# Halved matmul operands stored by even and odd tokens and read in turn, in a macaron decoder trunk on one Trainium2 core

## The chip, the cores and the metric

The kernel runs on one core of one Trainium2 chip. The metric is the device time of the whole program in microseconds (us), the median of several executions. Where engines are named, PE is TensorE's matmul side and PEld its weight loading, DVE is VectorE, ACT is ScalarE, POOL is GpSimd, and SP is the engine that issues most of the transfers.

## What is computed

Two layers, each made of a half-step SwiGLU feed-forward block, a mixer with three head groups, and a second half-step feed-forward block. There are 512 tokens, the model is 1024 wide and the feed-forward blocks 2816. Of the reference, what matters here:

```python
def swiglu(h, w_in, w_out):
    gate, up = jnp.split(h @ w_in, 2, axis=-1)
    return (jax.nn.silu(gate) * up) @ w_out
...
for l in range(DEPTH):
    x = x + 0.5 * swiglu(rms_norm(x, ffn1_norm[l]), ffn1_w_in[l], ffn1_w_out[l])
    h = rms_norm(x, mix_norm[l]) @ w_mix_in[l]
    (c_x, c_b, c_c, h_q, h_f, h_i, h_g, f_q, f_k, f_v, f_f) = jnp.split(h, split_at, axis=-1)
    y = jnp.concatenate([short_conv_mixer(...), hgrn2_mixer(...), fox_mixer(...)], axis=-1)
    x = x + y @ w_mix_out[l]
    x = x + 0.5 * swiglu(rms_norm(x, ffn2_norm[l]), ffn2_w_in[l], ffn2_w_out[l])
```

Everything is float32.

## The kernel before

**Three matmuls for one product.** Each float32 operand is split into a rounded part `hi` (type fp32r) and the rest `lo`; a product is then hi·hi + hi·lo + lo·hi, three fp32r matmuls into one accumulator. `mm3` (lines 423 to 437) issues the three, so its lines 428, 434 and 435 are most of the matmuls of the program. A matmul has a *stationary* operand of 128 columns, put into the array by a weight load that the profile lists as LDWEIGHTS under PEld, and a *moving* operand whose columns stream past it; both are read from SBUF, the on-chip memory. Each of the three matmuls has a weight load of its own, which runs while the matmul before it streams.

**Reading in turn.** `woven` (line 184) rewrites the moving operand: a row of 512 columns is read as column 0, column 256, column 1, column 257 and so on, two halves 1024 bytes apart read in turn. The accumulator then holds the columns in this order, and whoever reads the accumulator uses `unwoven` (line 194), which takes every second column, beside `halves` (line 189) for the tensor in ordinary order. `woven` does so only where the operand has T = 512 columns; narrower operands are read straight through.

**Halved products.** In the feed-forward blocks, most of both projections is computed by a seven-product scheme on 2x2 blocks: the tokens are cut into two halves of H = 256, the contraction and the features into two each, and sums and differences of the quarters are multiplied. The method `halved` (lines 825 to 1019) runs them; `plan` (line 66) writes out the order of the products and, for each place in it, which transfers, sums and operands are made there. One call of `product` (lines 907 to 917) is 2 feature groups by 4 contraction blocks by 3 matmuls, that is 24 matmuls, each with 256 moving columns. The stationary operands are weights: `prepare` makes their `hi` on ACT (line 882) and their `lo` on DVE (line 884) three products ahead, into one of three buffers named `hl`. The moving operands are of two kinds, both made once by `two` (lines 810 to 820), `hi` on ACT and `lo` on DVE: `xc`, seven per feed-forward block, from the normalised input quarters `xn` (made by `operand`), and `m`, fourteen per block, from the hidden quarters `hq` (made by `moving`). Before, each is a tile of 4 contraction blocks by 256 tokens in ordinary token order. With `follow`, the order of instructions on PE, ACT, DVE and SP around these products is set by hand: an instruction on an engine waits for the one before it in this order.

**Skew.** The buffer `hl` starts its contents 16 elements late where it is the stationary operand of a halved product (`SKEW_HELD`) and 48 elements late where it is a moving operand narrower than 512 columns (`SKEW_MOVING`).

**Mixer.** The 264 columns are the 256 columns of `H_I` (the values of the linear-recurrence heads) and the 8 columns of `F_F` (the forget gates of the attention heads), computed together at line 1162 with the tokens as the stationary and the weights as the moving operand, in four steps of two contraction blocks per layer. The weights of a step come by two transfers on SP's queue into one of two buffers `st` (`load_rows`, line 352), are split by lines 413 and 416, and the results are taken from the accumulators at lines 1169 and 1172.

**Last output.** The last feed-forward block leaves its result with tokens on the partitions, weights moving; the last tile of 512 columns is cut into two halves of 256 so that its end comes sooner (lines 616 to 656).

Of the kernel before, what the change touches and what calls it, by code (L numbers as in the profile page):

```python
# [182 lines left out]

def woven(x):

    return x.rearrange("p (h t) -> p t h", h=2) if x.shape[-1] == T else x


def halves(x):
# [9 lines left out]
class Trunk:  # L199
# [223 lines left out]
    def mm3(self, acc, ah, al, bh, bl, first, last, parted=False, keep=False):  # L423

        nc = self.nc
        n = bh.shape[-1]
        for c in (slice(0, n // 2), slice(n // 2, n)) if parted else (slice(0, n),):
            i = nc.tensor.matmul(  # L428
                acc[:, c], ah, woven(bh[:, c]), start=first and c.start == 0, stop=False,
                skip_group_check=True,  # L430
            )
            if keep:
                self.follow("p", i)
        nc.tensor.matmul(acc, ah, woven(bl), start=False, stop=False, skip_group_check=True)  # L434
        i = nc.tensor.matmul(acc, al, woven(bh), start=False, stop=last, skip_group_check=True)  # L435
        if keep:
            self.follow("p", i)

# [159 lines left out]
    def ffn(self, w_in, w_out, next_gain, covered, mean=None, begin=None, out=None):  # L598

        nc = self.nc
        tc = self.tc
        with tc.tile_pool(name=self.n("ffn"), bufs=1) as fp:
            self.tt, self.tb = "g2", 2
            if begin is not None:
                x, gain = begin
            self.hq = {}
            self.cover(fp, w_in, w_out, covered, mean, begin)

            f0, nf = CHUNKS[-1]
            if next_gain is not None:
                self.begin_norm(next_gain)
            last = out is not None
            self.ntog += 1
            if last:
                xs = []
                turn = self.turn_x(xs, (("mm", "mm"), ("sc", "pt"))[self.ntog % 2])
            for dg in range(2):
                banks = self.next4()  # L620

                def parts(k, kk, dg=dg):
                    r = slice((f0 + k) * P, (f0 + k + kk) * P)
                    return [w_out[r, dg * 512 : (dg + 1) * 512]]

                spans = [slice(c, c + P) for c in (0, 128, 256, 384)]
                jobs = [
                    (bk, slice(0, T), c) if last else (bk, c, None) for bk, c in zip(banks, spans)
                ]
                pieces = [[(bk, slice(0, T))] for bk in banks]  # L630
                if last and dg:

                    pieces[3] = [
                        (bk[:, : T // 2], slice(c, c + T // 2))
                        for bk, c in ((banks[3], 0), (self.next4()[0], T // 2))
                    ]
                    jobs[3:] = [(bk, c, spans[3]) for bk, c in pieces[3]]
                for _ in self.stream_steps(
                    jobs,
                    parts, lambda k: (self.hh[k // 2][:, k % 2, :], self.hl[k // 2][:, k % 2, :]), nf,  # L640
                ):
                    if last:
                        next(turn, None)
                if last:
                    for i in range(4):
                        o = self.xo[dg * 4 + i]
                        for bk, c in pieces[i]:
                            whole = c.stop - c.start == T
                            nc.vector.scalar_tensor_tensor(
                                out=halves(o[:, c]), in0=unwoven(bk) if whole else halves(bk),  # L650
                                scalar=0.5, in1=halves(xs[dg * 4 + i][:, c]),
                                op0=ALU.mult, op1=ALU.add,
                            )
                            nc.sync.dma_start(
                                out[0, spans[i], dg * T + c.start : dg * T + c.stop], o[:, c]
                            )
                    continue
                for i in range(4):
                    j = dg * 4 + i
                    xj = self.xT[:, j, :]  # L660
                    nc.vector.scalar_tensor_tensor(
                        out=halves(xj), in0=unwoven(banks[i]), scalar=0.5, in1=halves(xj),
                        op0=ALU.mult, op1=ALU.add,
                    )
                    if next_gain is not None:
                        self.norm_part(j, fp)
# [133 lines left out]
    def operand(self, fp, name):  # L800

        c = ORDER_IN.index(name)
        hi, lo = (
            fp.tile([P, 4, T // 2], F32R, tag=f"x{w}{c}", name=self.n("xc")) for w in "hl"
        )
        a, v = self.two(hi, lo, self.xn[SUM[name]], name in NEGATIVE)
        self.follow("a", a), self.follow("v", v)
        self.xc[name] = hi, lo

    def two(self, hi, lo, src, other):  # L810

        nc = self.nc
        if other:
            return (
                nc.scalar.activation(hi, src, AF.Copy, scale=-1.0),
                nc.vector.scalar_tensor_tensor(
                    out=lo, in0=src, scalar=-1.0, in1=hi, op0=ALU.mult, op1=ALU.subtract
                ),
            )
        return nc.scalar.copy(hi, src), nc.vector.tensor_sub(lo, src, hi)  # L820

    def halved(self, fp, w_in, w_out, covered, deal):
# [63 lines left out]
        def moving(c, p):  # L886

            hi, lo = (
                fp.tile([P, 4, H], F32R, tag=f"m{w}", name=self.n("m"), bufs=2) for w in "hl"
            )  # L890
            a, v = self.two(hi, lo, self.quarter(fp, c, *SUM[p]), p in NEGATIVE)
            A(a), V(v)
# [13 lines left out]

        def product(u, p, bank, start, stop, parted):
            hi, lo = parts.pop((u, p))
            xh, xl = self.xc[p] if u[0] == "I" else mov[u[1][0], p]
            for i in range(2):  # L910
                acc, c = bank[:, i * H : (i + 1) * H], slice(i * P, (i + 1) * P)
                for k in range(4):
                    self.mm3(
                        acc, hi[:, k, c], lo[:, k, c], xh[:, k, :], xl[:, k, :],
                        start and i == 0 and k == 0, stop and i == 1 and k == 3,
                        parted and i == 0 and k == 0, True,
                    )
# [158 lines left out]
    def mix(self, l, w, w_out, conv_w, out_gain, q_gain, k_gain, f_bias, next_gain, logits):  # L1076
# [3 lines left out]
        with tc.tile_pool(name=self.n("mix"), bufs=1) as mp:  # L1080
# [48 lines left out]
            with tc.tile_pool(name=self.n("hg"), bufs=1) as hp:  # L1129
# [28 lines left out]
                for i in range(2):  # L1158
# [2 lines left out]
                bv = [self.bank(t) for t in ("mm", "sc", "sc", "mm")]  # L1161
                self.stream(
                    [(bv[i][:, :264], slice(0, 264), TOK[i]) for i in range(4)],
                    cols((H_I, 256), (F_F, 8)), self.xact, KD,
                )
                v = hp.tile([P, 4, 256], F32, tag="v", name=self.n("v"))
                zf = mp.tile([P, 4, NH], F32, tag="zf", name=self.n("zf"))
                for i in range(4):
                    nc.scalar.activation(
                        v[:, i, :], bv[i][:, :256], AF.Copy, scale=self.invc[:, i : i + 1]  # L1170
                    )
                    nc.vector.scalar_tensor_tensor(
                        out=zf[:, i, :], in0=bv[i][:, 256:264], scalar=self.invc[:, i : i + 1],
                        in1=fb, op0=ALU.mult, op1=ALU.add,
                    )
                run = [
                    self.hgrn(l, pr, hp, z[pr], q[pr], v, sg[pr], og, S[pr], kb[pr], b[pr])
# [705 lines left out]
```

## Time and profile before

| | |
|---|---|
| median of 3 runs | 1788.92 us (1787.59 to 1790.13) |
| the profiled execution, its own time | 1787.5 us |
| its span in the profile | 1785.7 us |
| instructions in the profile | 33379 |
| bytes read from device memory over the span | 226.15 MB, 128 GB/s |

The page of the profile gives busy time by engine, then the span in 40 slices, the transfers, and the chain of work that ended last. Matmuls are pipelined: the time of one, as listed, runs from its start to the end of its last result, so it overlaps the next one, and the rate at which a stretch runs is read from the distance between the starts of successive matmuls. In the lists of groups a line reads: line of the kernel, engine, operation, what it writes and reads, partitions by elements, count, then the busy time of the group, the mean time of one in ns, and the engine's idle time before them with what ended it. In the view by windows each row has a stretch, its length, and for each engine the busy time with the number of instructions in brackets.

### The profile page before, as it was taken

How to read it: one execution, taken by the hardware profiler on the slowest of the kernel's cores; microseconds unless marked ns; L12 is line 12 of the kernel's file. 1: busy time of each engine (PE TensorE's matmuls, PEld its weight loads, DVE VectorE, ACT ScalarE, POOL GpSimd, SP SyncE). 2: the span in 40 equal slices, each digit the busy share in tenths (PEclk: the TensorE clock that was granted, in tenths of full speed). 3: DMA queues.
4: the chain of work that ended last, by engine and by line, in shares of the span. 5: the costliest groups of instructions: out<-in, count | busy, mean ns of one | idle time of the engine just before them, and what ended most of it. 6: DMA issues, size and time to landing. Idle time of an engine off the chain costs nothing.

```text
span 1785.7 us, 33379 instructions
## 1 busy us (share of the span) xinstructions
PE 1774.0 (99%) x13613; PEld 1659.7 (93%) x13613; DVE 1428.7 (80%) x1991; ACT 993.9 (56%) x1417; POOL 176.8 (10%) x174
## 2 busy tenths in 40 slices
PE   9999999999999999999999999999999999999999
PEld 7999999888888899999989999998878889999998
DVE  8889887678777888879678887876777779888883
ACT  5555555465666565555445555555656655555552
POOL 0011120100000101112001110201000000020210
PEclk9999999999999999999999999999999999999999
DMA  7668784243543857868276787823435438687762
GB/s 216 185 132 190 182 175 104 76 116 92 131 110 107 239 138 156 198 158 175 83 209 139 169 184 194 170 76 80 123 91 128 119 108 211 166 163 193 156 140 95
DMA packets 253114, 262.35 MB, mean 147 GB/s; under 512 B 23528, under 2 KB 232176, under 8 KB 252960
## 3 DMA queue, kind: packets, MB, share of 16 engines
q1 hardware_dynamic: 197104, 192.02, 35.7%
q0 software_dynamic: 55840, 68.19, 23.9%
q8 instruction: 107, 1.75, 0.4%
q14 instruction: 47, 0.39, 0.1%
q10 hardware_dynamic: 16, 0.00, 0.0%
HBM read 226.15 MB, written 2.17 MB: 128 GB/s over the span
## 4 chain that ended last, share of the span: by engine, by line
PE 87%; DVE 6%; ACT 4%; DMA 2%; issue 1%; SPq 0%; ACTq 0%; DVEq 0%
PE mm L428 13%; PE mm L435 12%; PE mm L434 12%; PE sc L428 6%; PE sc L435 6%; PE sc L434 6%; PE pt L428 6%; PE pt L434 6%; PE pt L435 6%; PE po L428 3%; PE po L434 3%; PE po L435 3%; DVE hl L416 2%; ACT hl L413 1%; DMA st<-in_ffn_w_in_dram 1%
## 5 line engine op out<-in xcount | busy, mean ns | idle before, releaser
L882 ACT CAST hl<-w 128x1024 fp32r<-128x1024 f32 x322 | 337.7, 1050 | 341.9 <-PE mm L435 83.1
L884 DVE TENSOR_TENSOR hl<-w,hl 128x1024 fp32r<-128x1024 f32 x322 | 392.6, 1220 | 83.1 <-ACT hl L882 82.9
L416 DVE TENSOR_TENSOR hl<-st,hl 128x1024 fp32r<-128x1024 f32 (+3 forms) x152 | 160.1, 1053 | 108.7 <-ACT hl L413 107.9
L413 ACT CAST hl<-st 128x1024 fp32r<-128x1024 f32 (+3 forms) x151 | 137.7, 912 | 166.3 <-PE po L435 78.4
L428 PE MATMUL mm<-xc,hl 128*128 128x256 f32 (+1 forms) x730 | 201.3, 276 | 0.3 <-ACT g L981 0.3
L435 PE MATMUL mm<-xc,hl 128*128 128x256 f32 x728 | 201.2, 276 | 0.0
L434 PE MATMUL mm<-xc,hl 128*128 128x256 f32 x728 | 201.1, 276 | 0.0
L428 PE MATMUL sc<-xc,hl 128*128 128x256 f32 (+1 forms) x530 | 146.4, 277 | 0.6 <-ACT g L981 0.6
L435 PE MATMUL sc<-xc,hl 128*128 128x256 f32 x528 | 146.1, 277 | 0.1
L434 PE MATMUL sc<-xc,hl 128*128 128x256 f32 x528 | 146.0, 277 | 0.0
L428 PEld LDWEIGHTS mm<-xc,hl 128*128 128x128 f32 x730 | 137.1, 188 | 0.8 <-ACT g L981 0.5
L435 PEld LDWEIGHTS mm<-xc,hl 128*128 128x128 f32 x728 | 136.7, 188 | 0.1
L434 PEld LDWEIGHTS mm<-xc,hl 128*128 128x128 f32 x728 | 136.7, 188 | 0.0
L434 PE MATMUL pt<-xc,hl 128*128 128x256 f32 x480 | 132.6, 276 | 0.0
L428 PE MATMUL pt<-xc,hl 128*128 128x256 f32 (+1 forms) x482 | 132.6, 276 | 0.0
L435 PE MATMUL pt<-xc,hl 128*128 128x256 f32 x480 | 132.5, 276 | 0.0
L428 PE MATMUL mm<-x,hl 128*128 128x512 f32 x272 | 105.9, 389 | 0.0
L435 PE MATMUL mm<-x,hl 128*128 128x512 f32 x272 | 103.1, 379 | 0.0
L434 PE MATMUL mm<-x,hl 128*128 128x512 f32 x272 | 103.1, 379 | 0.0
L428 PEld LDWEIGHTS sc<-xc,hl 128*128 128x128 f32 x530 | 99.5, 188 | 1.4 <-ACT g L981 1.0
L435 PEld LDWEIGHTS sc<-xc,hl 128*128 128x128 f32 x528 | 99.2, 188 | 0.3 <-DVE hl L884 0.3
L434 PEld LDWEIGHTS sc<-xc,hl 128*128 128x128 f32 x528 | 99.1, 188 | 0.0
(506 smaller groups left out, 5404.8 us busy)
## 6 DMA issues: line engine op xcount, KB each, us to landing
w<-in_ffn_w_in_dram SPq DMA_DIRECT2D x140, 512.0 KB, 5.4
w<-in_ffn_w_out_dram SPq DMA_DIRECT2D x64, 512.0 KB, 5.5
w<-in_ffn_w_out_dram POOLq DMA_DIRECT2D x56, 512.0 KB, 8.5
st<-in_w_mix_in_dram SPq DMA_DIRECT2D x80, 256.0 KB, 3.0
w<-in_ffn_w_in_dram POOLq DMA_DIRECT2D x39, 512.0 KB, 8.4
st<-in_ffn_w_in_dram SPq DMA_DIRECT2D x70, 256.0 KB, 3.6
w<-S POOLq DMA_DIRECT2D x35, 512.0 KB, 4.8
st<-in_ffn_w_out_dram SPq DMA_DIRECT2D x24, 512.0 KB, 3.6
```

The source lines that it names most:

```text
L413: a = nc.scalar.copy(hi, src[:, c : c + w])
L416: b = nc.vector.tensor_sub(lo, src[:, c : c + w], hi)
L428: i = nc.tensor.matmul(acc[:, c], ah, woven(bh[:, c]), start=first and c.start == 0, stop=False, skip_group_check=True,)
L434: nc.tensor.matmul(acc, ah, woven(bl), start=False, stop=False, skip_group_check=True)
L435: i = nc.tensor.matmul(acc, al, woven(bh), start=False, stop=last, skip_group_check=True)
L882: A(nc.scalar.copy(hi, src))
L884: return lambda: V(nc.vector.tensor_sub(lo, src, hi))
```

## The change

The moving operands `xc` and `m` are stored as two rows of 512: first all even tokens of all four contraction blocks, then all odd ones. `two` reads its source with a step of two elements for this and writes straight through. `product` views the operand as contraction block by token by half, and `mm3` reads it so that the two halves, 2048 bytes apart, come in turn; the columns then arrive in ordinary token order, and whoever reads these accumulators is unchanged. `woven` now applies to every moving operand that is a plain row of columns, whatever its width; so the 264 columns (halves 528 bytes apart) and the two last output halves (512 bytes apart) are read in turn as well, and their readers use `unwoven`. For the 264 columns the weights are brought in an order that puts half of `H_I` and half of `F_F` together, by four transfers a step.

```diff
 def woven(x):
 
-    return x.rearrange("p (h t) -> p t h", h=2) if x.shape[-1] == T else x
+    return x.rearrange("p (h t) -> p t h", h=2) if len(x.shape) == 2 else x
...
     def mm3(self, acc, ah, al, bh, bl, first, last, parted=False, keep=False):
 
         nc = self.nc
-        n = bh.shape[-1]
+        n = acc.shape[-1]
+        bh, bl = woven(bh), woven(bl)
         for c in (slice(0, n // 2), slice(n // 2, n)) if parted else (slice(0, n),):
             i = nc.tensor.matmul(
-                acc[:, c], ah, woven(bh[:, c]), start=first and c.start == 0, stop=False,
-                skip_group_check=True,
+                acc[:, c], ah, bh[:, c.start // 2 : c.stop // 2, :],
+                start=first and c.start == 0, stop=False, skip_group_check=True,
             )
             if keep:
                 self.follow("p", i)
-        nc.tensor.matmul(acc, ah, woven(bl), start=False, stop=False, skip_group_check=True)
-        i = nc.tensor.matmul(acc, al, woven(bh), start=False, stop=last, skip_group_check=True)
+        nc.tensor.matmul(acc, ah, bl, start=False, stop=False, skip_group_check=True)
+        i = nc.tensor.matmul(acc, al, bh, start=False, stop=last, skip_group_check=True)
...
                         for bk, c in pieces[i]:
-                            whole = c.stop - c.start == T
                             nc.vector.scalar_tensor_tensor(
-                                out=halves(o[:, c]), in0=unwoven(bk) if whole else halves(bk),
+                                out=halves(o[:, c]), in0=unwoven(bk),
...
         hi, lo = (
-            fp.tile([P, 4, T // 2], F32R, tag=f"x{w}{c}", name=self.n("xc")) for w in "hl"
+            fp.tile([P, 2, T], F32R, tag=f"x{w}{c}", name=self.n("xc")) for w in "hl"
         )
...
     def two(self, hi, lo, src, other):
 
         nc = self.nc
+        src = src.rearrange("p k t -> p (k t)").rearrange("p (n h) -> p h n", h=2)
         if other:
...
             hi, lo = (
-                fp.tile([P, 4, H], F32R, tag=f"m{w}", name=self.n("m"), bufs=2) for w in "hl"
+                fp.tile([P, 2, T], F32R, tag=f"m{w}", name=self.n("m"), bufs=2) for w in "hl"
             )
...
         def product(u, p, bank, start, stop, parted):
             hi, lo = parts.pop((u, p))
-            xh, xl = self.xc[p] if u[0] == "I" else mov[u[1][0], p]
+            xh, xl = (
+                x.rearrange("p h (k t) -> p k t h", k=4)
+                for x in (self.xc[p] if u[0] == "I" else mov[u[1][0], p])
+            )
...
-                        acc, hi[:, k, c], lo[:, k, c], xh[:, k, :], xl[:, k, :],
+                        acc, hi[:, k, c], lo[:, k, c], xh[:, k], xl[:, k],
...
                     [(bv[i][:, :264], slice(0, 264), TOK[i]) for i in range(4)],
-                    cols((H_I, 256), (F_F, 8)), self.xact, KD,
+                    cols((H_I, 128), (F_F, 4), (H_I + 128, 128), (F_F + 4, 4)), self.xact, KD,
                 )
...
                     nc.scalar.activation(
-                        v[:, i, :], bv[i][:, :256], AF.Copy, scale=self.invc[:, i : i + 1]
+                        halves(v[:, i, :]), unwoven(bv[i][:, :256]), AF.Copy,
+                        scale=self.invc[:, i : i + 1],
                     )
                     nc.vector.scalar_tensor_tensor(
-                        out=zf[:, i, :], in0=bv[i][:, 256:264], scalar=self.invc[:, i : i + 1],
-                        in1=fb, op0=ALU.mult, op1=ALU.add,
+                        out=halves(zf[:, i, :]), in0=unwoven(bv[i][:, 256:264]),
+                        scalar=self.invc[:, i : i + 1], in1=halves(fb), op0=ALU.mult, op1=ALU.add,
                     )
```

On every engine the same instructions stand in the same order as before; only SP's queue has more of them, eight transfers more in each layer.

## The prediction

> **What bounds the kernel now.** I read the busy shares first, then the chain that ended last.
>
> ```profile
> PE 1774.0 (99%) x13613; PEld 1659.7 (93%) x13613; DVE 1428.7 (80%) x1991; ACT 993.9 (56%) x1417; POOL 176.8 (10%) x174
> ...
> PEclk9999999999999999999999999999999999999999
> ...
> PE 87%; DVE 6%; ACT 4%; DMA 2%; issue 1%; SPq 0%; ACTq 0%; DVEq 0%
> ```
>
> PE is the bound, at the full granted clock throughout. Since busy matmuls overlap, 99% says only that PE rarely waits; what it could gain is in the spacing of starts. The halved products fill four stretches, one per feed-forward block:
>
> ```profile
> 76.50:305.20 228.70, 228.70 (x2018) 228.67 (x2017) 193.60 (x203) 128.33 (x145) 32.22 (x27) 1.00 0.71 158
> 616.80:865.70 248.90, 248.53 (x2185) 247.97 (x2184) 213.34 (x226) 140.04 (x160) 35.36 (x30) 1.00 0.71 158
> 939.40:1188.00 248.60, 248.29 (x2186) 247.84 (x2185) 212.39 (x225) 139.52 (x159) 34.43 (x29) 1.00 0.71 158
> 1498.40:1747.10 248.70, 248.39 (x2186) 248.00 (x2186) 213.44 (x225) 138.79 (x159) 35.32 (x30) 1.00 0.71 159
> sum 974.90, PE 973.92 PEld 972.48 DVE 832.76 ACT 546.69 POOL 137.33; mean PE 243.48 PEld 243.12 DVE 208.19 ACT 136.67 POOL 34.33
> ```
>
> The columns are PE, PEld, DVE, ACT, POOL. Together 2018 + 2185 + 2186 + 2186 = 8575 matmuls in 974.9 us, 113.7 ns each; PE idles 1 us in all, DVE is busy 85%, ACT 56%. Inside, the spacing is constant (timeline: start, length, both us):
>
> ```profile
> 119.95 0.28 PE L435 MATMUL po<-xc,hl 128*128 128x256 f32 x1
> ...
> 122.67 0.28 PE L435 MATMUL mm<-xc,hl 128*128 128x256 f32 x1
> ```
>
> That is 24 spacings in 2.72 us: 113.3 ns for 256 columns. The operands of 512 columns, already read in turn, do better per column:
>
> ```profile
> 354.69 0.38 PE L435 MATMUL mm<-x,hl 128*128 128x512 f32 x1
> ...
> 368.29 0.38 PE L435 MATMUL mm<-x,hl 128*128 128x512 f32 x1
> ```
>
> 63 spacings in 13.60 us: 215.9 ns for 512 columns, so 107.9 for 256. The question is whether those 113.3 ns belong to the order of reading.
>
> **Halved products: order of reading.** One place streams rows straight through with almost no weight load beside them (8 columns):
>
> ```profile
> 399.37 0.39 PE L1534 MATMUL pt<-utri,flh 128*8 128x512 f32 x1
> 399.60 0.40 PE L1534 MATMUL pt<-utri,fll 128*8 128x512 f32 x1
> ...
> 400.18 0.28 PE L1534 MATMUL pt<-utri,flh 128*8 128x256 f32 x1
> 400.29 0.28 PE L1534 MATMUL pt<-utri,fll 128*8 128x256 f32 x1
> 400.41 0.22 PE L1534 MATMUL pt<-utri,flh 128*8 128x128 f32 x1
> ```
>
> Straight through, 512 columns take 230 ns (399.37 to 399.60) against 215.9 in turn, and 256 take 115 (400.18 to 400.41, two). So straight reading costs 6 to 7% by itself, without a weight load to blame, and the 113.3 is of the same kind. I take it that reading in turn removes it.
>
> How far down? The stream itself allows half of 215.9, 107.9, if nothing in a matmul is fixed; what is fixed would add a little.
>
> The Trainium skill, "TensorE: Matmul & The Clock Gate", section "Wait — 56ns, not 53.3ns?", states columns over 2.4 GHz plus about 2.5 ns a matmul; the 215.9 agrees, and by it alone the halved products would run at 109.2 and gain 35 us.
>
> From the side of the weight load, which in the halved products never rests (two rows of the timeline, then two groups: count, busy us, mean ns):
>
> ```profile
> 519.15 0.23 PE L1714 MATMUL po<-PH,V 128*128 128x128 f32 x1
> 519.21 0.27 PE L1714 MATMUL po<-PL,V 128*128 128x128 f32 x1
> ...
> L1714 PE MATMUL po<-PL,V 128*128 128x128 f32 x32 | 8.8, 274 | 0.0
> L1714 PE MATMUL po<-PH,V 128*128 128x128 f32 x32 | 7.2, 224 | 0.0
> ```
>
> Here 128 columns stream for less time than a load takes: the second matmul starts 60 ns after the first and ends 60 + 274 - 224 = 110 ns after it, so back-to-back loads allow about 110 ns. Does reading in turn slow the load beside it?
>
> ```profile
> L428 PEld LDWEIGHTS mm<-xc,hl 128*128 128x128 f32 x730 | 137.1, 188 | 0.8 <-ACT g L981 0.5 <-issue 0.2
> L428 PEld LDWEIGHTS mm<-x,hl 128*128 128x128 f32 x272 | 51.5, 189 | 7.7 <-issue 1.0
> ```
>
> 188 ns beside straight reading, 189 beside reading in turn, and such a load lies within each of the 215.9 ns, beside the stream, as one would always do after the change. The trace has no pair 2048 bytes apart, only 1024. The slower of stream and load sets the pace, so I take the load's 110, less a little because its starts are given in steps of 10 ns: 109.6, and 8575 x (113.3 - 109.6) = 32 us. Bounds: 107.9 gives 46, 110 gives 28, and with the load at fault nothing.
>
> **What the writers pay.** `two` now reads every second element; ACT and DVE each do it for 32 + 24 + 16 + 12 = 84 operands:
>
> ```profile
> L820 ACT CAST m<-hq 128x1024 fp32r<-128x1024 f32 x32 | 33.4, 1044 | 2.8 <-DVE hq L897 2.8
> L815 ACT ACTIVATE m<-hq 128x1024 fp32r<-128x1024 f32 x24 | 25.2, 1051 | 0.0
> L820 ACT CAST xc<-xn 128x1024 fp32r<-128x1024 f32 x16 | 16.7, 1041 | 5.5 <-DVE xn L719 4.1 <-DVE xn L793 1.4
> L815 ACT ACTIVATE xc<-xn 128x1024 fp32r<-128x1024 f32 x12 | 12.7, 1059 | 8.5 <-DVE xn L719 5.5 <-DVE xn L793 3.0
> ...
> L324 ACT ACTIVATE lk<-lk 128x512 f32<-128x512 f32 x4 | 2.5, 635 | 6.0 <-DVE lk L1317 6.0
> L324 ACT ACTIVATE t<-lk 128x256 f32<-128x256 f32 x4 | 2.0, 588 | 0.0
> ```
>
> ```profile
> L1397 DVE TENSOR_TENSOR t<-t,q 128x256 f32<-128x256 f32 x4 | 1.5, 420 | 0.0
> L1404 DVE TENSOR_TENSOR t<-kb,b 128x256 f32<-128x256 f32 x20 | 8.3, 415 | 0.0
> ```
>
> On DVE the step of two costs nothing (L1397 reads and writes with that step, L1404 in runs). On ACT, `t<-lk` reads and writes with a step of two: 588 ns, where 256 straight elements would take some 430 (635 less 256 at the 0.80 ns between the 512 and the 1024 row). If all of that excess lies in the reading, an operand costs 4 x 158 = 0.63 us more. I take a quarter, 0.16, since half the stepping there is writing, and nothing shows a stepped read alone. In both cases ACT has room: at worst 84 x 0.63 = 53 us on 547. The wait falls on DVE, where `lo` stands right behind in the given order and everything after it waits too, the `lo` of the next weights first. DVE then has 833 + 53 = 886 us of 943, 94%; the three products that are prepared ahead cover that on the mean, and not everywhere. They already ran out once:
>
> ```profile
> 838.58 0.19 PEld L435 LDWEIGHTS sc<-xc,hl 128*128 128x128 f32 x1 [0.26 <-DVE hl L884]
> ```
>
> I set 3 us of PE waiting against the gain; bounds 0 and 15, the latter a quarter of the 53 plus 2.
>
> **The 264 columns.** 372.12 to 373.32 holds ten spacings:
>
> ```profile
> 372.12 0.28 PE L435 MATMUL sc<-hl,x 128*128 128x264 f32 x1
> ...
> 373.32 0.29 PE L428 MATMUL sc<-hl,x 128*128 128x264 f32 x1
> ```
>
> 120 ns each; at the 512 rate 111.3. With 96 a layer, 192 x 8.7 = 1.7 us gained, if PE is what waits last. Against it stands the queue of SP, with eight issues more a layer (a row of the timeline, then a group with ACT's idle time before it).
>
> ```profile
> 372.52 0.88 SPq L352 DMA_DIRECT2D st<-in_w_mix_in_dram  x2
> ...
> L413 ACT CAST hl<-st 128x528 fp32r<-128x528 f32 x8 | 4.9, 617 | 0.6 <-DMA st<-in_w_mix_in_dram 0.6
> ```
>
> An issue takes 0.44 us, so the last part of a step is issued 0.88 us later, and the loads of the next projection stand behind it. The cast already waited for such a transfer. Cost between 0 and 8 x 0.88 = 7 us; I take 2, most steps being loaded ahead. Net: nothing. The two last output halves are 36 matmuls:
>
> ```profile
> L428 PE MATMUL pt<-hl,hh 128*128 128x256 f32 x6 | 1.7, 284 | 0.0
> ```
>
> 36 x (284 - 271) = 0.5 us, 271 being 379 less 108. Their DVE readers take every second element of an accumulator, as those of the other banks do already.
>
> **Sum.** -32 + 3 + 0 - 0.5 = -29.5 us on the execution's own 1787.5, 1758. The shown median is 1.4 us higher than that execution: 1759.
>
> **Rivals.**
>
> *The load sets the 113.3 (no change).* PEld is 93% busy, and 113.3 is only 3 ns above what loads allow. Against it: the rows with 8-column loads show the cost of straight reading without a load. Time: 1789, to 1792 with the writers' waits. Chance 0.06; I count 113.3 to 112.9 here.
>
> *DVE takes over (half the gain).* Stepped reads cost ACT the full 0.63 us and DVE's order passes it on. For: DVE at 85%, above 90% where a block's operands are made. Against: lookahead of three products. Time: 1759 + 12 = 1771. Chance 0.13.
>
> *Reading in turn collides with the weight load (slower).* A load that never rests may meet both halves, which 512 columns with a load in only half of the time do not show. Price: straight rows of 256 against another placement of the weights run at 120 ns,
>
> ```profile
> 518.67 0.28 PE L1714 MATMUL po<-PH,V 128*128 128x256 f32 x1
> ...
> L1659 PE MATMUL sc<-S,S 128*128 128x256 f32 x8 | 2.7, 333 | 0.0
> ```
>
> four spacings in 0.48 us from there to the 519.15 above; so 8575 x 6.7 = 57 us more, 1846. The worst placement in the trace takes 333 ns a matmul, 57 over the 276 that the halved ones take; that would be 489 us. It decides as soon as the spacing ends above 113.3. Against it: 189 for the load, 215.9 for the stream, with both on. The Trainium skill, "SBUF — State Buffer", section "Specifications (TRN2)", speaks for this rival: lines have 16 bytes, and full bandwidth wants at least two hits per line, while reading in turn leaves the line at every element. By that rule 512 columns in turn should already be the slower ones; the trace has them at 215.9 against 230, so it does not hold for this stream. Chance 0.08.
>
> **Chances and range.** The forecast has 0.73: 1742 (spacing 107.9, no waits) to 1768 (spacing 110, waits at 8). With DVE taking over it reaches 1777. I leave out the slower rival and most of no change: 1746 to 1777. Faster by more than 0.2% (3.6 us, about what a measurement of this kernel can tell): 0.73 + 0.13 = 0.86, less 0.01 for waits that eat more than the gain; same 0.06; slower 0.08 + 0.01 = 0.09.
>
> **What would show it.** In the changed profile, 256-column matmuls of lines 428 to 436 at 271 or 272 ns instead of 276, their spacing 109 to 110, and stretches of about 241 us with the same counts; PEld still 188 to 190. For the writers, the `m` and `xc` casts on ACT between 1.04 and 1.68 us and DVE's wait for them (4.8 us for `m<-hq` in before); PE waiting for `hl` L884 in more than one place. For the mixer, 264-column spacing at 111 to 112 and the idle time of the 128x528 cast. I am wrong if the spacing stays above 112, or if it falls and PE waits for DVE take more than 10 us.

## The result, and the profile after

The changed kernel takes 1779.89 us (median of 6 runs, 1779.45 to 1781.39) against 1788.89 us for the kernel before in the same comparison: 9.0 us less, a ratio of 0.995 with a 95% interval of 0.9937 to 0.9963. That is faster by 0.5%, which a measurement of this kernel can tell from nothing, but less than a third of the 29.5 us that was forecast, and outside the range given. One execution in all that follows, the third of run 12, ran at a granted clock of 0.556 and took 3022.88 us; it is counted in that run's median of 1779.82 us, which is 1779.61 us without it, and not in its ratio.

The page of the changed kernel: busy shares, granted clock, chain that ended last.

```profile
PE 1761.0 (99%) x13613; PEld 1644.1 (92%) x13613; DVE 1439.3 (81%) x1991; ACT 1022.1 (57%) x1417; POOL 176.9 (10%) x174
...
PEclk9999999999999999999999999999999999999999
...
PE 81%; DVE 10%; ACT 5%; issue 2%; DMA 2%; SPq 0%; ACTq 0%; DVEq 0%
```

PE is still the bound at the full clock; ACT and DVE hold a little more of the chain. The four stretches of halved products, cut at the first and last start of a halved matmul in each kernel, by the view of busy time in windows (length, then PE, PEld, DVE, ACT, POOL). The changed kernel:

```profile
77.60:304.20 226.60, 226.26 (x2020) 225.67 (x2020) 195.80 (x203) 132.19 (x145) 32.23 (x27) 1.00 0.72 159
615.60:862.80 247.20, 245.48 (x2187) 244.54 (x2187) 215.70 (x227) 144.98 (x160) 36.45 (x31) 1.00 0.72 160
936.20:1183.10 246.90, 245.51 (x2188) 244.55 (x2187) 214.87 (x226) 144.49 (x160) 34.92 (x30) 1.00 0.71 160
1494.10:1741.40 247.30, 245.55 (x2188) 244.59 (x2187) 215.88 (x226) 143.81 (x159) 36.41 (x31) 1.00 0.71 160
sum 968.00, PE 962.79 PEld 959.35 DVE 842.25 ACT 565.48 POOL 140.01; mean PE 240.70 PEld 239.84 DVE 210.56 ACT 141.37 POOL 35.00
```

The kernel before, cut in the same way:

```profile
sum 976.10, PE 975.12 PEld 973.64 DVE 833.96 ACT 547.09 POOL 137.73; mean PE 243.78 PEld 243.41 DVE 208.49 ACT 136.77 POOL 34.43
```

The stretches are 8.1 us shorter, the three long ones some 247 us each in place of the 241 that were to show. PE now idles 5.2 us in them (968.00 less 962.79) where it idled 1.0. Two rows of the changed kernel's timeline give the spacing inside:

```profile
119.96 0.28 PE L436 MATMUL po<-xc,hl 128*128 128x256 f32 x1
...
122.64 0.28 PE L436 MATMUL mm<-xc,hl 128*128 128x256 f32 x1
```

24 spacings in 2.68 us: 111.7 ns, where before had 113.3 and 109.6 was forecast. Over the start-to-start times of all 8556 neighbouring halved matmuls in the records, leaving out the places where PE waits, the mean went from 113.41 to 111.67 ns. Groups of the kernel before and of the changed one (count, busy us, mean ns, idle us before):

```profile
L435 PE MATMUL mm<-xc,hl 128*128 128x256 f32 x728 | 201.2, 276 | 0.0
```

```profile
L435 PE MATMUL mm<-xc,hl 128*128 128x256 f32 x728 | 200.3, 275 | 0.0
...
L435 PEld LDWEIGHTS mm<-xc,hl 128*128 128x128 f32 x728 | 139.8, 192 | 0.0
```

A matmul lasts 275 ns where it lasted 276, not the 271 or 272 expected, and a weight load 192, which is above the 188 to 190 expected. These rows, with the 111.7, are the first sign that the load and not the stream sets the pace now.

The casts that make the operands, first one of the kernel before, then those of the changed one:

```profile
L820 DVE TENSOR_TENSOR m<-hq,m 128x1024 fp32r<-128x1024 f32 x32 | 39.1, 1221 | 4.9 <-ACT m L820 4.8
```

```profile
L821 ACT CAST m<-hq 128x1024 fp32r<-128x1024 f32 x32 | 43.6, 1363 | 3.2 <-DVE hq L898 3.2
...
L821 ACT CAST xc<-xn 128x1024 fp32r<-128x1024 f32 x16 | 24.7, 1545 | 6.6 <-DVE xn L719 6.2 <-DVE xn L793 0.4
...
L821 DVE TENSOR_TENSOR m<-hq,m 128x1024 fp32r<-128x1024 f32 x32 | 43.2, 1350 | 9.8 <-ACT m L821 9.8
...
L821 DVE TENSOR_TENSOR xc<-xn,xc 128x1024 fp32r<-128x1024 f32 x16 | 23.1, 1446 | 4.6 <-ACT xc L821 4.6
```

On ACT the `m` cast went from 1044 to 1363 ns and the `xc` cast from 1041 to 1545; DVE, which was taken to pay nothing, went from about 1220 to 1350 and 1446. Its wait for ACT's `m` doubled (4.8 to 9.8 us). What PE waits for in the halved products, from the view of waits (us in total, times, longest of one); first the kernel before, then the changed one:

```profile
PE sc L428 <- ACT g L981: 0.6, 2, 0.3
...
PE mm L428 <- ACT g L981: 0.3, 1, 0.3
```

```profile
PE sc L429 <- ACT g L985: 2.3, 2, 1.2
...
PE mm L429 <- ACT g L985: 0.8, 1, 0.8
...
PE mm L436 <- DVE hl L885: 0.6, 2, 0.3
PE sc L436 <- DVE hl L885: 0.6, 2, 0.3
...
PE sc L429 <- DVE u L991: 0.4, 2, 0.2
...
PE mm L429 <- DVE u L991: 0.3, 1, 0.3
```

PE waits mostly near the entry of a block, for an accumulator that ACT must first copy out (line 985), and near its end for the weights' `lo` (line 885). Counted as start-to-start time above the undisturbed spacing, these waits grew from 3.9 us in 39 places to 10.7 us in 52.

So in the stretches: 8556 x 1.74 ns = 14.9 us won by the spacing, 6.7 us given back to waits, 8.2 left. The profiled executions differ by only 6.1 us, because the first halved product started 1.3 us later in this one and the second mixer took 0.9 longer; in the runs below, whose opening is nearly the same, that start lies anywhere between 75.8 and 77.3 us, so this start is not counted as an effect of the change. The mixer is looked at in run 12.

### The profile page after: what moved, and what is told of

It is laid out like the page before. It is cut to its first block, busy times and chain, and to the rows that moved or that the text cites. A ratio compares the mean times of both kernels' runs of the same rounds, so it can differ in the third digit from the quotient of the medians.

```text
span 1779.6 us, 33419 instructions
## 1 busy us (share of the span) xinstructions
PE 1761.0 (99%) x13613; PEld 1644.1 (92%) x13613; DVE 1439.3 (81%) x1991; ACT 1022.1 (57%) x1417; POOL 176.9 (10%) x174
## 4 chain that ended last, share of the span: by engine, by line
PE 81%; DVE 10%; ACT 5%; issue 2%; DMA 2%; SPq 0%; ACTq 0%; DVEq 0%
PE mm L429 11%; PE mm L436 11%; PE mm L435 11%; PE pt L435 5%; PE pt L436 5%; PE pt L429 5%; PE sc L436 5%; PE sc L429 5%; PE sc L435 5%; PE po L429 3%; PE po L435 3%; PE po L436 3%; DVE hl L416 2%; DVE hl L885 2%; ACT hl L413 1%
## 5 line engine op out<-in xcount | busy, mean ns | idle before, releaser
L416 DVE TENSOR_TENSOR hl<-st,hl 128x1024 fp32r<-128x1024 f32 (+3 forms) x152 | 160.1, 1054 | 108.9 <-ACT hl L413 107.9
L429 PEld LDWEIGHTS mm<-xc,hl 128*128 128x128 f32 x730 | 140.1, 192 | 2.0 <-ACT g L985 0.9
L436 PEld LDWEIGHTS mm<-xc,hl 128*128 128x128 f32 x728 | 139.8, 192 | 0.9 <-DVE hl L885 0.9
L435 PEld LDWEIGHTS mm<-xc,hl 128*128 128x128 f32 x728 | 139.8, 192 | 0.0
L429 PEld LDWEIGHTS sc<-xc,hl 128*128 128x128 f32 x530 | 101.7, 192 | 4.1 <-ACT g L985 2.7
L436 PEld LDWEIGHTS sc<-xc,hl 128*128 128x128 f32 x528 | 101.4, 192 | 0.9 <-DVE hl L885 0.9
L435 PEld LDWEIGHTS sc<-xc,hl 128*128 128x128 f32 x528 | 101.4, 192 | 0.0
```

Source lines behind the costliest of these rows:

```text
L416: b = nc.vector.tensor_sub(lo, src[:, c : c + w], hi)
L429: i = nc.tensor.matmul(acc[:, c], ah, bh[:, c.start // 2 : c.stop // 2, :], start=first and c.start == 0, stop=False, skip_group_check=True,)
L435: nc.tensor.matmul(acc, ah, bl, start=False, stop=False, skip_group_check=True)
L436: i = nc.tensor.matmul(acc, al, bh, start=False, stop=last, skip_group_check=True)
```

## The experiments

The question was why the spacing stopped at 111.7. All spacings in this section are means over the records of the halved matmuls.

**1 and 2: the three matmuls of a product given different parts.** In both kernels the second matmul of `mm3` keeps a full stream of 256 columns but holds 64 weight columns; the third keeps a full load of 128 but streams 128 columns. Weight load and stream of one place can then be told apart. (Shown as in the changed kernel.)

```diff
-        nc.tensor.matmul(acc, ah, bl, ...)
-        i = nc.tensor.matmul(acc, al, bh, ...)
+            nc.tensor.matmul(acc[:64], ah[:, :64], bl, ...)
+            i = nc.tensor.matmul(acc[:, :128], al, bh[:, :64, :], ...)
```

> The kernel before, with two of the three matmuls of a halved product cut down: the second has only 64 of its 128 stationary columns, the third streams only 128 of its 256 moving columns (its results are left incomplete). So one trace gives three spacings: a 256-column stream beside a load of 64 columns, a 256-column stream beside a load of 128, and a 128-column stream beside a load of 128. Theory L (weight load sets the pace only after the change): 113 for the first two, since straight reading by itself costs that, and 109 to 111 for the third, the bare load. Theory S (the load never matters, the stream does): 113, 113 and well under 107 for the third. If the load set the pace already before: under 111 for the first, 113 for the other two.

> The changed kernel, cut in the same way. Theory L (after the change the pace is the weight load's): 108 to 109.5 for a 256-column stream beside a load of 64 columns, 111.7 beside a load of 128, and 111 to 112 for a 128-column stream beside a load of 128. Theory S (a pair 2048 bytes apart streams at 111.7 by itself): 111.7, 111.7, and under 110 for the third. Theory C (stream and load collide): 109 for the first, 111.7 for the second, under 110 for the third.

Measured: 1805.32 us straight and 1774.2 in turn. From the second matmul (short load, full stream) to the third: 118.3 ns straight, 109.1 in turn. So a stream in turn whose own load was short does run at 109, as theory L of run 2 had it. The 118.3 is more than any theory of run 1 had, and it stays unexplained. The first matmul, which follows a stream of only 128 columns, waits for its load: it lasts 332 ns straight and 328 in turn, 56 and 53 more than normal. Its start lies 60 and 58 ns after the start of the one before, so with the wait the distance is 116 and 111 ns. That the load is about as long as the stream was plain from this; how long to a nanosecond was not. Runs 8 and 9 ask it more directly.

**3: the writers alone.** The operands are stored by even and odd tokens as in the changed kernel, but streamed straight through.

```diff
-                x.rearrange("p h (k t) -> p k t h", k=4)
+                x.rearrange("p h (k t) -> p k h t", k=4)
```

> The changed kernel, but the halved operands, though stored by even and odd tokens, are read straight through (columns then arrive in another order, so the results are wrong). Spacing 113.3 and the stepped casts stay. If the growth of PE's waits (3.8 to 10.6 us in excess spacing) comes from the stepped casts on ACT and DVE: 1791 to 1795 us. If it comes from PE being faster: waits as before, 1788 to 1790. Both expect casts of 1.37 to 1.55 us on ACT.

Measured: 1789.54 us, a ratio of 0.9999 (0.9989 to 1.0009) to the kernel before, with the spacing at 113.5. With PE reading straight, the stepped casts cost the program nothing. Groups of this run:

```profile
L823 ACT CAST m<-hq 128x1024 fp32r<-128x1024 f32 x32 | 36.3, 1134 | 2.8 <-DVE hq L900 2.8
...
L823 DVE TENSOR_TENSOR m<-hq,m 128x1024 fp32r<-128x1024 f32 x32 | 39.2, 1224 | 6.2 <-ACT m L823 5.9
...
L823 ACT CAST xc<-xn 128x1024 fp32r<-128x1024 f32 x16 | 24.0, 1499 | 6.1 <-DVE xn L721 5.6 <-DVE xn L795 0.4
...
L823 DVE TENSOR_TENSOR xc<-xn,xc 128x1024 fp32r<-128x1024 f32 x16 | 22.8, 1426 | 3.8 <-ACT xc L823 3.8
```

The same `m` instructions with the same stepped reads take 1134 ns on ACT here and 1363 in the changed kernel; on DVE 1224 and 1350. The difference beside them is how PE reads at the time. The `xc` rows seem to speak against this: 1499 and 1426 here, nearly what the changed kernel shows. But these groups mix two places. Most `xc` casts are made at the entry of a block, where PE reads its 512 columns in turn in this run too. The 18 casts on ACT that lie wholly beside such matmuls take 1586 ns on the mean, the nine that lie beside the halved matmuls, here straight, 1139; on DVE it is 1521 (15 casts) and 1224 (12). So most of what the stepped casts pay is not the step but the step beside PE reading in turn. Both theories had expected ACT's casts at 1.37 to 1.55 us in this run; for `m` that was missed.

**4: even and odd put apart at the source.** The tensors `xn` and `hq` are written by even and odd tokens where the accumulators and the normalised input are read, so that the casts run straight again; the matmuls are those of the changed kernel.

```diff
-        src = src.rearrange("p k t -> p (k t)").rearrange("p (n h) -> p h n", h=2)
...
-                out=t[:, k, :], in0=self.xT[:, i, b * H : (b + 1) * H],
+                out=t[:, :, P * k : P * k + P], in0=unwoven(self.xT[:, i, b * H : (b + 1) * H]),
...
-                A(nc.scalar.activation(g1, acc, AF.Copy, scale=-1.0))
+                A(nc.scalar.activation(halves(g1), unwoven(acc), AF.Copy, scale=-1.0))
```

> The changed kernel, with even and odd tokens put apart earlier, where results leave the accumulators and where the input is normalised, so that ACT's and DVE's casts read straight again. Spacing 111.7 as in the changed kernel, casts 1.04 us on ACT and 1.22 on DVE. If the stepped casts cause the added waits: waits back to about 4 us, 1772 to 1775 us. If a faster PE causes them: 1778 to 1781.

Measured: 1778.83 us, ratio 0.9938 (0.9924 to 0.9953), which is what was expected if a faster PE causes the waits. The casts are back at their old times, and part of the cost has moved to the writing of `xn` (480 ns in run 3):

```profile
L820 ACT CAST m<-hq 128x1024 fp32r<-128x1024 f32 x32 | 33.4, 1045 | 3.3 <-DVE hq L897 3.3
...
L793 DVE SCALAR_TENSOR_TENSOR xn<-xT,ngain,inv 128x256 f32<-128x256 f32 x32 | 16.3, 587 | 0.0
```

The spacing is again 111.67, and the waits of PE fall only from 10.7 to 8.7 us. So taking the step out of the casts wins back 2.0 of the 6.7 us of added waits. That the other 4.8 come with a faster PE, which is sooner at an accumulator or a weight tile that ACT and DVE release at their old pace, is argued and not shown by this run alone, since its writing of `xn` is slower. Two other runs support it: with the stepped casts and a PE that reads straight the waits are 4.4 us (run 3), and with the casts of the changed kernel and a PE that is faster still they are 12.8 us (run 9). In time this version is the lowest measured here with the whole computation, but its interval overlaps that of the changed kernel, so it is not shown to be better.

**5, 6 and 7: where the weights lie.** The weights of the halved products begin 64 bytes away from the moving operands, modulo 256. If load and stream met in the same places of the memory, another offset would change the load.

```diff
-SKEW_HELD, SKEW_MOVING = 16, 48
+SKEW_HELD, SKEW_MOVING = 0, 48
```

(and 32 and 48 in place of 0)

> The changed kernel with the held weights moved by 64 bytes (16 columns), so that weights and moving operands of the halved products begin at the same place of a 256-byte line of addresses, as the 512-column products have it (there the load takes 189 ns). Theory C (the load is lengthened by a meeting of addresses that the placement decides): load 188 to 189, spacing 109 to 110, time 1768 or less. Theory F (a load beside reading in turn is paced at 111.7 wherever the weights lie): load 192, spacing 111.5 to 112, time 1779 to 1782.

> The changed kernel with the held weights moved the other way, 128 bytes from the moving operands instead of 64. Theory C: the load and the spacing differ from the 192 and 111.7 of the changed kernel, in either direction, by more than 1 ns. Theory F: 192, 111.5 to 112, 1779 to 1782.

> As before with 192 bytes between weights and moving operands. Theory C: differs from 192 and 111.7 by more than 1 ns, in either direction. Theory F: 192, 111.5 to 112, 1779 to 1782.

Measured: 1780.69, 1781.16 and 1779.67 us, spacing 111.67 in all three, and one row for all, from run 5:

```profile
L435 PEld LDWEIGHTS mm<-xc,hl 128*128 128x128 f32 x728 | 139.9, 192 | 0.0
```

The placement is not it: theory F holds in all three.

**8 and 9: short loads, full streams.** In both kernels the second and third matmul of three hold only 64 weight columns, for three of the four contraction blocks; every stream keeps its 256 columns. Half of all loads are then short.

```diff
+        if keep == 2:
+            nc.tensor.matmul(acc[:64], ah[:, :64], bl, ...)
+            acc, al = acc[:64], al[:, :64]
```

> The kernel before with the second and third matmul of three (for three of the four k) holding only 64 of their 128 weight columns, so that two of three loads are half as long; the other 64 rows of those products are left out. If straight reading itself costs the 113.4 (the prediction's reason): all spacings stay at 113 to 114, time 1786 to 1790. If the weight load set the 113.4: the spacings ahead of a short load fall to 110 or less, time 1770 or less.

> The same cut in the changed kernel. Theory L (the load of 128 columns sets the 111.7 and the stream in turn alone would run at 109): spacings ahead of a short load 109 to 109.5, half of the products' time from about 966 to some 950 us and 1764 to 1770 in all. Rival (the 111.7 belongs to the stream, with its pairs 2048 bytes apart): 111.7 everywhere, 1779 to 1782.

Measured, straight: 1787.84 us. The rows are two loads, full and short, and two places of the timeline with 26 spacings between them:

```profile
L428 PEld LDWEIGHTS mm<-xc,hl 128*128 128x128 f32 x730 | 137.0, 188 | 0.8 <-ACT g L987 0.5 <-issue 0.2
...
L435 PEld LDWEIGHTS mm<-xc,hl 128*64 128x64 f32 x546 | 73.2, 134 | 0.0
```

```profile
119.73 0.28 PE L435 MATMUL po<-xc,hl 128*64 128x256 f32 x1
...
122.68 0.28 PE L428 MATMUL mm<-xc,hl 128*128 128x256 f32 x1
```

2.95 us over 26 is 113.5 ns, in short and full loads alike (113.3 to 113.6 by kind). Loads of half the columns, 134 ns for 188, change nothing: reading straight through cost the 113.4, as the prediction had it.

Measured, in turn: 1772.44 us. The loads, and two places of the timeline with nine spacings between them, all in blocks with short loads:

```profile
L429 PEld LDWEIGHTS mm<-xc,hl 128*128 128x128 f32 x730 | 138.5, 190 | 2.3 <-ACT g L991 1.0 <-ACT g L984 0.7 <-issue 0.5
...
L436 PEld LDWEIGHTS mm<-xc,hl 128*64 128x64 f32 x546 | 75.3, 138 | 0.0
...
L441 PEld LDWEIGHTS mm<-xc,hl 128*128 128x128 f32 x182 | 34.9, 192 | 0.0
```

```profile
120.69 0.28 PE L429 MATMUL mm<-xc,hl 128*128 128x256 f32 x1
...
121.68 0.28 PE L429 MATMUL mm<-xc,hl 128*128 128x256 f32 x1
```

0.99 us over nine is 110.0 ns. By kind, a matmul with a short load is followed after 109.2 to 109.4 ns, one with a full load after 111.4 to 112.0. A matmul with a full load waits those 2 ns inside its own duration (276 or 275 against 273 ns), so the one behind it starts later. The 111.7 thus belongs to the full load of 128 columns, and the stream in turn runs at 109.3 once the load lets it. A matmul with 64 weight columns also writes only 64 rows of results, so one could put the 2 ns down to the results. Against that stand the 512-column matmuls, which read in turn and write all 128 rows: in the records of the changed kernel they start 215.8 ns apart (2823 spacings), 106.5 more than the 109.3, which leaves no 2 ns for the rows. The expected 1764 to 1770 was missed for two reasons: I had not counted that half of the loads stay full (mean spacing 110.42), and PE's waits grew again, to 12.8 us.

**10: weights in steps.** If straight addresses slow a stream, perhaps they slow a load too. A weight operand takes one step only, so the three matmuls took their 128 columns in steps of 2, 4 and 8 elements.

```diff
+                    h1 = hi[:, k].rearrange("p (c s) -> p s c", s=2)[:, i]
+                    h2 = hi.rearrange("p (g k) c -> p g (k c)", g=2)[:, j // 4]
+                    h2 = h2.rearrange("p (c s) -> p s c", s=4)[:, j % 4]
+                    l3 = lo.rearrange("p k c -> p (k c)").rearrange("p (c s) -> p s c", s=8)[:, j]
```

> The changed kernel with its 128 weight columns taken in steps of 2 (first matmul), of 4 (second) and of 8 elements (third), in place of 128 neighbours; the weights are stored as before, so the products are of other columns. Theory S (the load suffers from straight addresses as the stream did): the load of one or more of the three lines falls to 188 or less, and the spacing ahead of it to 109 to 110. Rival N (addresses do not matter to a load): 192 and 111.7 in all three, 1779 to 1782. If stepping hurts a load: spacings above 113 and 1790 or more.

Measured: 2511.75 us. The three loads, in steps of 8, 4 and 2:

```profile
L437 PEld LDWEIGHTS mm<-xc,hl 128*128 128x128 f32 x728 | 245.5, 337 | 0.0
...
L436 PEld LDWEIGHTS mm<-xc,hl 128*128 128x128 f32 x728 | 227.1, 312 | 0.0
...
L429 PEld LDWEIGHTS mm<-xc,hl 128*128 128x128 f32 x730 | 159.1, 218 | 0.1
```

Theory S and rival N both fell; stepping hurts a load: 218 ns for a step of 2 and 312 and 337 for 4 and 8, against 192. The three spacings, counted from the matmuls with steps of 2, 4 and 8, became 121, 233 and 241 ns. The loads are 26, 120 and 145 ns longer and the spacings 9, 122 and 129, so longer loads are paid for, nearly in full where they are long. This is one more sign that the load sets the pace here.

**11: pairs 512 bytes apart.** The trace of before had pairs 1024 bytes apart only, and the change made them 2048.

```diff
-                x.rearrange("p h (k t) -> p k t h", k=4)
+                x.rearrange("p h t -> p (h t)").rearrange("p (k h t) -> p k t h", k=4, h=2)
```

> The changed kernel with the two tokens that are read in turn 512 bytes apart instead of 2048 (the operands are stored as before, so columns meet other columns). Theory D (the distance of 2048 is what lengthens the load and holds the spacing): load 188 to 189, spacing 109 to 110, 1768 or less. Rival N: load 192, spacing 111.7, 1779 to 1782.

Measured: 1781.35 us, spacing 111.67, loads 192 ns, as rival N had it. The distance, 512 or 2048 bytes, does not change the load's pace; what it does to a stream with a short load was not run.

**12: the second part undone.** Only the halved products keep the change; the 264 columns and the last output halves are as before.

```diff
-    return x.rearrange("p (h t) -> p t h", h=2) if len(x.shape) == 2 else x
+    return x.rearrange("p (h t) -> p t h", h=2) if x.shape[-1] == T else x
...
-                    cols((H_I, 128), (F_F, 4), (H_I + 128, 128), (F_F + 4, 4)), self.xact, KD,
+                    cols((H_I, 256), (F_F, 8)), self.xact, KD,
```

> The changed kernel with its second part undone: the 264 columns in the order, the cutting of transfers and the reading of before, and the two last output halves read straight through; only the halved products keep the change. The prediction's step (the second part is worth 1.7 and 0.5 us of stream and costs some 2 us of SP's queue, so net nothing): 1780 to 1782, 264-column spacing back at 120, idle time of the 128x528 cast back at 0.6 us. If the second part by itself lost time: 1775 to 1778. If it won more than forecast: 1783 or more.

Measured: 1779.82 us, ratio 0.9947 (0.9934 to 0.996), against 1779.89 with the second part, and just under the 1780 to 1782 of the prediction's step. Its effect is nothing within the measurement. First the changed kernel's rows (the 264-column stream with 13 spacings, and the cast), then those of this run (8 spacings, and the cast):

```profile
370.79 0.28 PE L435 MATMUL sc<-hl,x 128*128 128x264 f32 x1
...
372.25 0.28 PE L436 MATMUL sc<-hl,x 128*128 128x264 f32 x1
...
L413 ACT CAST hl<-st 128x528 fp32r<-128x528 f32 x8 | 5.0, 626 | 1.7 <-DMA st<-in_w_mix_in_dram 1.4 <-ACT qe L324 0.2
```

```profile
370.95 0.28 PE L429 MATMUL sc<-hl,x 128*128 128x264 f32 x1
...
371.91 0.28 PE L436 MATMUL mm<-hl,x 128*128 128x264 f32 x1
...
L413 ACT CAST hl<-st 128x528 fp32r<-128x528 f32 x8 | 4.9, 618 | 0.5 <-DMA st<-in_w_mix_in_dram 0.5
```

112.3 ns against 120.0: the columns are read faster with the change, some 1.5 us over the 192 matmuls, and the cast idles 1.7 us, mostly for its cut transfers, in place of 0.5. But a cast that waits is not yet PE that waits. What PE pays stands in its own waits; of the changed kernel:

```profile
PE mm L429 <- DVE zf L1177: 1.9, 2, 1.4
```

Neither the kernel before nor run 12 has such a row. PE comes sooner to the next use of the accumulators of the 264 columns and waits until `zf` has been read from them. DVE is hardly later there: in the first layer it starts on `zf` 18.30 us after its `lk` of line 1322 in the changed kernel (362.86 to 381.16) and 18.14 in run 12 (361.97 to 380.11). So gain and loss meet at these accumulators, once per layer.

## Why the prediction was wrong

| term | forecast, us | measured, us |
|---|---|---|
| spacing of the halved products | -32 (113.3 to 109.6) | -14.9 (113.41 to 111.67) |
| PE's waits for ACT and DVE | +3, bounds 0 and 15 | +6.7 |
| 264 columns | 0 (1.7 won, 2 lost) | 0 (1.5 won, 1.9 lost in waits for `zf`) |
| last output halves | -0.5 | -0.3 (last stretch 38.5 to 38.2) |
| sum | -29.5 | -8.5; medians -9.0 |

**That straight reading costs the 113.3: right.** Short loads leave it at 113.4 (run 8), and reading in turn lowers it whatever the offset or distance. The rival in which the load sets the 113.3 is out by the same run.

**What the stream allows: right.** The prediction bounded it by 107.9 and, with something fixed in each matmul, a little more. Runs 2 and 9 have 109.1 to 109.4. The Trainium skill, "TensorE: Matmul & The Clock Gate", section "Wait — 56ns, not 53.3ns?", gives columns over 2.4 GHz plus about 2.5 ns, by which 109.2 is the estimate for 256, and these runs agree with it.

**"From the side of the weight load ... about 110 ns": the step that failed.** The mechanism was the right one, that the slower of stream and load sets the pace, and the load was named as the one. Its size was wrong by 1.7 ns, or 2.1 from the 109.6 that was then used, and at 8556 spacings that is 14 to 18 us. The 110 was worked out from one pair of starts in a view that rounds to 10 ns (60 ns apart), with the mean durations 224 and 274. In the records of the same trace there are 32 such pairs; their starts lie 61.0 ns apart on the mean, and from the end of the first to the end of the second it is 108 to 114, mean 111.5. The ends of matmuls are modelled in these profiles, so the mean is worth more than any one pair. This was in the trace of before. It would have given 111.5 and a gain of 8556 x 1.9 = 16 us from the spacing. Runs 9 and 10 show that it is the load that holds the 111.7, by shorter and by longer loads. The further step from 110 down to 109.6 "because its starts are given in steps of 10 ns" took rounding as a reason to lean one way, when it left the whole 60 uncertain by 10. With that, the load's bound was no bound: 110 was used as the upper end.

The Trainium skill, "TensorE: Matmul & The Clock Gate", section "LDWEIGHTS (loading the stationary operand)", puts a load at its columns over 1.2 GHz, by which the estimate for 128 is 106.7 ns. The runs differ: full loads come 111.7 ns apart, 5.0 more, and by that figure the stream would have stayed the limit at 109.2.

**That reading in turn does not slow the load: open.** The prediction compared 188 with 189 ns. After the change the row says 192, behind a full load; behind a short one it is 189 (runs 2 and 9). Whether the 192 is a slower load or one that begins to count while the load ahead of it still runs, these runs do not tell. It may not be needed for the 111.7, since the straight pairs of before already have 111.5.

**The writers: sizes off, waits inside the bounds.** ACT pays 31.3 us over the 84 operands (32 x 319 + 24 x 327 + 16 x 504 + 12 x 431 ns), 0.37 us each, where 0.16 was taken and 0.63 the bound; DVE pays 13.6 us, where nothing was. What was missed is that the step costs more while PE reads in turn (run 3). The trace of before hid this on DVE: the instructions of line 1397, taken as proof that the step costs nothing, run from 399.28 to 400.04 us, almost wholly beside the very matmuls of line 1534 that stream straight. On ACT the two `t<-lk` stand beside 512 columns in turn, and their price of 0.63 us was nearer to the 0.54 that `xc` pays in such a place (1586 for 1046 ns) than the quarter that was taken. Taking the step out of the casts wins back only 2.0 us of waits (run 4). The bigger part, 4.8 us, was not in the sum as such: most likely waits for accumulators and weights that a slower PE did not have. They rise as the spacing falls: 3.9 us at 113.4, 10.7 at 111.7, 12.8 at 110.4.

**The rivals.** DVE did not take over: it is busy 842 us of 968, 87%. The collision that makes it slower did not happen: the spacing never rose. What came is a case that had no rival of its own: a load that stops the gain half way. Nor did the prediction's own sign of being wrong catch it, a spacing above 112 or waits for DVE of more than 10 us: the 111.7 fell between the 110 that was the worst of the forecast and the 112. That the change would be faster at all was given 0.86 and came true.

**The second part: right in its net, not in where it loses.** The 264 columns run at 112.3 ns for the 111.3 forecast, and the net is nothing (run 12). The loss was put at SP's queue. The cast's idle time did rise by 1.1 to 1.2 us, but PE loses its time at `zf`, a wait for which the sum had no term.

## What to carry to other kernels

Where two things run side by side at nearly the same pace, speeding up one wins only the distance to the other, and this distance has to be known better than the gain: take it as the mean over all places of the trace that show it, not from one pair of rounded starts, and lean no way on rounding. Take the price of an instruction from a row that has the same neighbours as the place that it is wanted for; here PE's way of reading beside it changed the price. With a weight load of 128 fp32r columns for every 256 moving columns reading in turn could not bring a matmul below 111.7 ns. And when the bounding engine gets faster, expect to give part of the gain back at places where it was just in time before: here 6.7 of 14.9 us, of which 4.8 remained with straight casts.

## What the runs showed of the hardware that was not expected

- Stepped reads on ACT and DVE depend on what PE does: the `m` cast takes 1044 ns straight, 1134 stepped while PE streams straight, and 1363 stepped while PE reads in turn; on DVE 1221, 1224 and 1350. Beside 512 columns in turn the stepped `xc` cast takes 1586 on ACT and 1521 on DVE (run 3). The straight casts do not depend on it (1045 beside reading in turn).
- A stream of 256 fp32r columns costs 113.4 ns straight and 109.1 to 109.4 in turn, with pairs 512 or 2048 bytes apart at the same pace of 111.7 under full loads. For a weight load it is the other way: steps of 2, 4 and 8 elements lengthen it from 192 to 218, 312 and 337 ns.
- A matmul that waits for its weights shows the wait in its own duration (332 against 276 ns in run 1, 397 and 404 against 275 in run 10), not as idle time before it. PE then counts as busy, and the views of waits of these runs do not name the load.
